# A seven-product step for half of the fourth column group of the down-projection, with sums made and split by halves

## The chip, the cores and the metric

The kernel runs on one core of a Trainium2 chip. The metric is the device time of one execution in microseconds (us), the median of several executions. In the profile PE is the matrix engine, PEld its weight loads, DVE the vector engine, ACT the scalar engine, POOL and SP the engines that here mostly issue transfers (DMAs).

## The reference

Two layers over 256 tokens of width 2048, in float32. The part that matters is the MLP at the end of each layer and the form of its products:

```python
for l in range(DEPTH):                       # DEPTH = 2, S = 256, D_MODEL = 2048, D_FF = 8192
    h = rms_norm(x, norm1_g[l])
    z = h @ w_in[l]                          # width 5120: q, k, v and two gMLP halves
    ...                                      # 8 attention heads, 8 gMLP groups -> mix
    x = x + mix @ w_out[l]
    h2 = rms_norm(x, norm2_g[l])
    x = x + jnp.square(jax.nn.relu(h2 @ w_up[l])) @ w_down[l]
return rms_norm(x, final_g)
```

## The kernel before

**Products.** Every float32 operand is split into a high part (a rounding to the matrix engine's fp32r type) and a low part (the remainder), and a product is made of three matmuls: high by high, low by high, high by low. A *weight tile* (class `Sub`) is 128 partitions x 1024 numbers: SP loads it (512 KB) into `raw`, ACT makes `hi` by a cast (L173), DVE makes `lo` by a subtraction (L183). A *plain* step (function `transposed`, matmuls of L415) uses one weight tile in 24 matmuls of 256 columns.

A *seven-product step* (function `fast`, matmuls of L443; the Strassen-Winograd form) takes four 256 x 256 blocks of weights, from two loaded tiles, `Top` and `Bottom`, and replaces two plain steps, 48 matmuls, by 42. For it DVE makes four weight differences of 128 x 512 (L224, L225, L228, L229), held in place of the raw tiles as two more tiles, `Sums`; these two get a cast and a low part like a plain tile (L173, L183), Top and Bottom a half-size cast (L191) and low part (L196) each. The matching combinations of the activations (`sum_parts`, kept in `shared`) are made once per eighth of the MLP: four DVE operations in `strassen_sums` (L485 to L488), then casts in `to_half` (ACT L661) and low parts (DVE L664).

**Stages.** The MLP is cut into eighths of 1024 hidden columns. Turn `e` of its loop (0 to 8), in the texts "eighth e", does the up-projection of eighth e, 16 plain steps numbered 0 to 15, and the down-projection of eighth e-1. After each four up steps ACT takes relu and square of 256 hidden columns (L888, L891) and casts them (L661), and DVE makes their low part (L664); so the last hidden columns of an eighth come at its step 15. The down-projection has four groups of 512 output columns. In eighths 1 to 6 three of them go by seven-product steps, two each (one per pair of row blocks of all 1024 rows), and the fourth by four plain steps, 16 to 19, whose results are added up in SBUF (L872, L875). In eighth 7 two groups are fast, in eighth 8 none.

**Results of the fast groups.** The seven products stay in PSUM for group 0; for the others ACT copies them out (three copies of 128 x 512, L1004, and one of 128 x 256, L990) and POOL's DMAs add them to the arrays `far` in DRAM (L969). In eighths 6 and 7 the last turn of a group is added the other way (L1000, L980 for group 0's seventh), `combine` adds the products up (seven DVE operations, L920 to L928, and ACT scalings, L933), `turn_back` turns each result on PE (four transposes, L945), and `update` adds it to `x` (L524).

**Order.** The program writes all engines' instructions from one list of steps. `ORDER` and `USUAL` say, per eighth and group, before which plain steps its fast steps stand. While step n is written, casts and low parts are written up to four tiles ahead (`high_to`, `low_to`); every engine runs its own instructions in the order written. A weight tile counts as a *unit*, so a fast step is four units; `soon`, `later` and `behind` put work off by units. PSUM banks are given in turn. The last two matmuls of a fast step are put into the next plain step.

## Time and profile before

| what | value |
|---|---|
| median of three runs | 2014.74 us (2014.72 to 2014.77) |
| profiled execution: own time, span | 2014.8 us, 2013.0 us |
| PE busy | 2000.5 us, 99% of the span, 16930 matmuls |
| DVE busy | 1659.6 us, 82%, 2116 instructions |
| ACT busy | 1259.3 us, 63%, 1695 instructions |
| bytes moved | 421.13 MB, mean 209 GB/s |

A line of instructions gives the start in us, the duration in us (of a run of several, from the first start to the last end), engine, line of the kernel, operation, output and inputs by name, shapes and count, then in brackets the idle time before it and what ended it. Durations of neighbours overlap, so what one instruction costs its engine is the distance from its start to the next one's, called pitch here. The windows view gives busy time and, in parentheses, instructions per engine, then the granted clock of PE.

### The profile page before, as it was taken

The numbers are of one execution on the slowest core, as the hardware profiler recorded it, in microseconds if no ns is written. First come the engines' busy times: TensorE is split into PE (matmuls) and PEld (weight loads), VectorE is DVE, ScalarE is ACT, GpSimd is POOL, SyncE is SP. The second block draws the span as 40 slices with busy tenths as digits, with TensorE's granted clock in tenths as the row PEclk, the third lists the DMA queues.
The fourth block names the chain that finished last, engine by engine and source line by source line (L and its number), as shares of the span: only waits on it lengthen the run. The fifth ranks groups of instructions, "written<-read, shape, count | busy, mean of one in ns | idle before, by whom it ended". The sixth has DMA issues, their size and how long they took to land.

```text
span 2013.0 us, 41185 instructions
## 1 busy us (share of the span) xinstructions
PE 2000.5 (99%) x16930; PEld 1971.9 (98%) x16930; DVE 1659.6 (82%) x2116; ACT 1259.3 (63%) x1695; POOL 136.8 (7%) x166
## 2 busy tenths in 40 slices
PE   9999999999999999999999999999999999999997
PEld 7999999999999999999989999999999999999997
DVE  7886866889888898898868877668888898888985
ACT  7666555676666666665647665556666666667653
POOL 0000300000001000100000003000001100010000
PEclk9999999999999999999999999999999999999998
DMA  8555556576678776876656456555677777778662
GB/s 325 199 170 166 189 191 208 165 263 211 206 230 241 242 222 202 245 218 214 201 176 209 167 173 196 189 193 180 240 233 218 231 235 216 235 223 251 200 215 82
DMA packets 127597, 421.13 MB, mean 209 GB/s; under 512 B 14256, under 2 KB 22448, under 8 KB 127408
## 3 DMA queue, kind: packets, MB, share of 16 engines
q1 hardware_dynamic: 110800, 389.86, 56.9%
q0 software_dynamic: 15456, 25.70, 7.1%
q8 instruction: 132, 2.16, 0.4%
q10 hardware_dynamic: 1152, 2.94, 0.4%
q14 instruction: 57, 0.47, 0.1%
HBM read 394.58 MB, written 23.86 MB: 208 GB/s over the span
## 4 chain that ended last, share of the span: by engine, by line
PE 99%; DMA 0%; DVE 0%; ACT 0%; ACTq 0%; issue 0%; DVEq 0%; SPq 0%
PE acc L415 69%; PE acc L443 12%; PE aux L443 9%; PE acc L475 2%; PE acc L474 2%; PE acc L473 2%; PE aux L772 0%; PE aux L650 0%; PE aux L608 0%; DMA raw<-in_w 0%; PE aux L637 0%; DMA x<-in_xT 0%; DVE x L1140 0%; PE aux L652 0%; PE acc L945 0%; PE aux L553 0%
## 5 line engine op out<-in xcount | busy, mean ns | idle before, releaser
L173 ACT ACTIVATE hi<-raw 128x1024 fp32r<-128x1024 f32 (+1 forms) x829 | 845.2, 1049 | 441.8 <-DVE raw L225 265.6
L183 DVE TENSOR_TENSOR lo<-raw,hi 128x1024 fp32r<-128x1024 f32 (+1 forms) x829 | 978.7, 1213 | 108.5 <-ACT hi L173 104.3
L415 PE MATMUL acc<-hs,hi 128*128 128x256 f32 x5632 | 988.6, 277 | 0.0
L415 PEld LDWEIGHTS acc<-hs,hi 128*128 128x128 f32 x5632 | 858.6, 188 | 0.4 <-issue 0.2
L415 PE MATMUL acc<-hs,lo 128*128 128x256 f32 x2816 | 778.0, 276 | 0.0
L415 PEld LDWEIGHTS acc<-hs,lo 128*128 128x128 f32 x2816 | 528.7, 188 | 0.4 <-issue 0.2
L415 PE MATMUL acc<-half,hi 128*128 128x256 f32 x2560 | 440.5, 276 | 0.0
L415 PEld LDWEIGHTS acc<-half,hi 128*128 128x128 f32 x2560 | 387.2, 188 | 0.0
L415 PE MATMUL acc<-half,lo 128*128 128x256 f32 x1280 | 353.3, 276 | 0.0
L415 PEld LDWEIGHTS acc<-half,lo 128*128 128x128 f32 x1280 | 240.3, 188 | 0.0
L969 POOL DMA_DIRECT2D far<-ar x100 | 80.9, 814 | 1138.1 <-ACT ar L972 519.2
L443 PE MATMUL acc<-hi,shared 128*128 128x256 f32 x832 | 149.9, 276 | 0.0
L443 PEld LDWEIGHTS acc<-hi,shared 128*128 128x128 f32 x832 | 129.1, 188 | 0.0
L443 PE MATMUL aux<-hi,half 128*128 128x256 f32 x608 | 126.4, 276 | 0.0
L443 PE MATMUL acc<-lo,shared 128*128 128x256 f32 x416 | 114.8, 276 | 0.0
L664 DVE TENSOR_TENSOR half<-ar,half 128x512 fp32r<-128x512 f32 x72 | 49.8, 691 | 63.7 <-ACT half L661 63.7
L443 PEld LDWEIGHTS aux<-hi,half 128*128 128x128 f32 x608 | 100.1, 188 | 0.0
L443 PE MATMUL acc<-hi,half 128*128 128x256 f32 x480 | 91.4, 276 | 0.0
L443 PE MATMUL aux<-lo,half 128*128 128x256 f32 x304 | 84.1, 277 | 0.0
L443 PE MATMUL aux<-hi,shared 128*128 128x256 f32 x448 | 80.7, 276 | 0.0
L524 DVE TENSOR_TENSOR x<-x,acc 128x512 f32<-128x512 f32 (+1 forms) x45 | 30.3, 674 | 58.9 <-PE acc L415 57.4
L443 PEld LDWEIGHTS acc<-lo,shared 128*128 128x128 f32 x416 | 78.1, 188 | 0.0
(181 smaller groups left out, 2113.4 us busy)
## 6 DMA issues: line engine op xcount, KB each, us to landing
raw<-in_w SPq DMA_DIRECT2D x731, 512.0 KB, 4.7
far<-ar POOLq DMA_DIRECT2D x66, 256.0 KB, 8.4
far<-ar POOLq DMA_DIRECT2D x34, 128.0 KB, 4.6
ar<-far POOLq DMA_DIRECT2D x12, 256.0 KB, 9.7
raw<-in_w SPq DMA_DIRECT2D x10, 256.0 KB, 5.0
x<-in_xT SPq DMA_DIRECT2D x7, 256.0 KB, 5.6
out<-x SPq DMA_DIRECT2D x7, 256.0 KB, 3.1
shared<-in_b_sp ACTq DMA_DIRECT2D x2, 512.0 KB, 7.5
```

Of the source, the lines that this page charges most:

```text
L173: act.activation(self.h[:, j * m:(j + 1) * m], self.raw[:, j * m:(j + 1) * m], AF.Copy)
L183: vec.tensor_tensor(lo[:, r], self.raw[:, r], self.h[:, r].bitcast(F32), op=OP.subtract)
L415: pe.matmul(o, lhsT=lhs, rhs=xs[:, rhs, :], start=(first and j == 0), stop=(last and j == 2), skip_group_check=True)
L443: calls.append(lambda k=k, j=j, lhs=lhs, rhs=rhs: pe.matmul(o[n], lhsT=lhs, rhs=rhs, start=(p == 0 and k == 0 and j == 0 and n in fresh), ...
L473: pe.matmul(ps, lhsT=xh, rhs=hi, start=(k0 + k == 0), stop=False)
L474: pe.matmul(ps, lhsT=xh, rhs=lo, start=False, stop=False)
L475: pe.matmul(ps, lhsT=xl, rhs=hi, start=False, stop=(k0 + k == KC - 1))
L524: vec.tensor_tensor(xj, xj, ps[j][:, 0:S] if alone else pair(ps)[:, j, :], op=OP.add)
L664: vec.tensor_tensor(t[:, c:c + 2, 1, :], src, t[:, c:c + 2, 0, :].bitcast(F32), op=OP.subtract)
L969: nc.gpsimd.dma_start(far[g][:, r], src, **({} if e == 1 else {"accum_op": OP.add}))
```

## The change

In eighths 1 to 5 the fourth group (output columns 1536 to 2047) is split by rows: the first 512 of the 1024 rows go by one seven-product step, before plain step 11, and the other 512 by two plain steps, 16 and 17, in place of four. For this the rows are paired in another way: a seven-product step now covers 512 neighbouring rows (top 256, bottom 256), and so does each half of the activation sums.

- The sums of the first half are made after step 8, and their casts and low parts behind the fast step that stands before plain step 14 (in eighth 6 before step 12); those of the second half follow step 15. Every low part of them is written one unit after its cast. Eighth 7's sums, which no step read, are no longer made.
- The hidden columns' first pair of blocks (of eighths 0 to 4) is cast and split for half of the tokens alone, since no plain step reads it any more.
- The products of the new step go out like those of group 1 and 2, into a fourth array `far[3]`, in eighths 1 to 5. In eighth 7, after group 0, one transfer of 128 x 1792 (0.92 MB) brings it into the tile `shared`; then come one `combine` and two `turn_back`s more per layer. The load of `far[0]` and group 0's `combine` stand four units later than before.
- The raw tiles are one tile with seven places, and the first two of the four weight differences become one operation of 128 x 1024 numbers; Bottom's low part stands behind it. Where a Top would take the last place, it and its Bottom change places.
- Group 2's fast steps stand before steps 14 and 15 (before: 13 and 14), and eighth 1 has the usual order.

The diff, cut to what matters:

```diff
@@ -60,10 +60,10 @@
-ORDER = {1: ((2, 5), (7, 8), (13, 14)), 6: ((12, 15), (2, 3), (7, 8)), 7: ((7, 10), (2, 3)), 8: ()}
-FINAL = (7, 7, 6)
+ORDER = {6: ((12, 15), (2, 3), (7, 8)), 7: ((7, 10), (2, 3)), 8: ()}
+FINAL = (7, 7, 6, 8)
 LAST = (4, 6, 8, 10, 0, 2, 12, 14)
-USUAL = ((7, 9), (2, 3), (13, 14))
+USUAL = ((7, 9), (2, 3), (14, 15), (11,))
@@ -147,6 +147,9 @@
+    raws = wp.tile([P, 1024 * RAW_BUFS], F32, name="raws")
@@ -158,7 +161,9 @@
         def load(self, parts):
-            self.raw = wp.tile([P, 1024], F32, name="raw", tag="raw", bufs=RAW_BUFS)
+            self.at = raw_at[0] % RAW_BUFS
...
+            self.raw = raws[:, 1024 * self.at:1024 * (self.at + 1)]
@@ -221,10 +226,13 @@
             if not self.second:
-                vec.tensor_tensor(t.left(), t.right(), t.left(), op=OP.subtract)
-                vec.tensor_tensor(t.right(), b.right(), t.right(), op=OP.subtract)
+                low_to(n_high[0] - 1)
+                o = t.raw.rearrange("p (k h n) -> p h k n", k=2, h=2)
+                right = raws.rearrange("p (s k h n) -> p s k h n", k=2, h=2, n=256)[:, t.at:b.at + 1:b.at - t.at, :, 1, :]
+                vec.tensor_tensor(o, right, o, op=OP.subtract)
...
             if not self.second:
+                low_to(n_high[0])
@@ -416,33 +424,33 @@
-    def fast(name, l, row0, col0, forms, slots, fresh, last, done):
+    def fast(name, l, row0, col0, forms, slots, fresh, last, done, count=2):
         o = []
-        for p in range(2):
-            top, bottom = (cls(name, l, row0 + (4 * h + 2 * p) * P, col0, 2, 512) for h, cls in enumerate((Top, Bottom)))
+        for p in range(count):
+            top, bottom = (cls(name, l, row0 + (4 * p + 2 * h) * P, col0, 2, 512) for h, cls in enumerate((Top, Bottom)))
...
                     o.extend(slots())
-                half, extra = forms()
+                half, extra = forms(p)
...
                     for k in range(2):
-                        xh, xl = (a[:, 4 * lower_rows + 2 * p + k, i, tt * P:(tt + 1) * P] for i in range(2))
+                        xh, xl = (a[:, 4 * p + 2 * lower_rows + k, i, tt * P:(tt + 1) * P] for i in range(2))
...
                                 o[n], lhsT=lhs, rhs=rhs, start=(p == 0 and k == 0 and j == 0 and n in fresh),
-                                stop=(n in last and p == 1 and k == 1 and j == 2), skip_group_check=True))
+                                stop=(n in last and p == count - 1 and k == 1 and j == 2), skip_group_check=True))
@@ -479,9 +487,12 @@
-    def strassen_sums(f, i, n):
...
-        a11, a12, a21, a22 = (f[:, 4 * k + i:4 * k + i + n, t * P:(t + 1) * P] for t in range(2) for k in range(2))
+    def strassen_sums(f, p=None):
...
+        f = f.rearrange("p (a r k) t -> p a r k t", a=2, r=2)
+        f = f if p is None else f[:, p:p + 1]
+        a11, a12, a21, a22 = (f[:, :, r, :, t * P:(t + 1) * P] if p is None else f[:, 0, r, :, t * P:(t + 1) * P]
+                              for t in range(2) for r in range(2))
@@ -656,12 +667,13 @@
-        def to_half(t, c, src, wait=False):
...
-            act.activation(t[:, c:c + 2, 0, :], src, AF.Copy)
+        def to_half(t, c, src, wait=False, n=S):
...
+            act.activation(t[:, c:c + 2, 0, 0:n], src[:, :, 0:n], AF.Copy)
             def low():
-                vec.tensor_tensor(t[:, c:c + 2, 1, :], src, t[:, c:c + 2, 0, :].bitcast(F32), op=OP.subtract)
+                vec.tensor_tensor(t[:, c:c + 2, 1, 0:n], src[:, :, 0:n], t[:, c:c + 2, 0, 0:n].bitcast(F32),
+                                  op=OP.subtract)
@@ -889,29 +901,33 @@
                 act.activation(z, z, AF.Square)
-                to_half(hid[e][0], c // P, z, True)
-                if e == 0 and c == 512:
+                to_half(hid[e][0], c // P, z, True, P if e < 5 and c == 0 else S)
+                if e == 0 and c == 256:
...
                     sum_parts[0] = shared[0].rearrange("p (k h t) -> p k h t", k=NH, h=2)
-                    later(1, 1.0, lambda: sums([0]))
-                if c == 768:
-                    summed[0] = False
-                    later(1, 1.5, lambda: sums([0, 1] if e else [1]))
+                if c % 512 == 256 and e < 7:
+                    if c == 768:
+                        later(1, 1.0, lambda: strassen_sums(inner, 1))
+                        parts(1, 1)
+                    elif e == 0:
+                        later(1, 1.0, lambda: strassen_sums(inner, 0))
+                        parts(0, 1)
...
-        def sums(ps):
...
-            strassen_sums(inner, 2 * ps[0], 2 * len(ps))
...
-            def parts(k):
-                to_half(sum_parts[0], k, inner[:, k:k + 2, :])
-                summed[0] = k == 6
...
-            for k in range(0, 8, 2):
-                if k % 4 // 2 in ps:
-                    later(0, 0.6, lambda k=k: parts(k))
...
-        def combine(place, c, banks, o=None):
+        def parts(p, wait):
+            summed[p] = wait is None
...
+            def part(k):
+                to_half(sum_parts[0], k, inner[:, k:k + 2, :], True)
+                summed[p] = summed[p] or k % 4 == 2
...
+            for k in (4 * p, 4 * p + 2):
+                if wait is None:
+                    part(k)
+                else:
+                    later(wait, 0.6, lambda k=k: part(k))
...
+        def combine(place, c, banks, o=None, between=2):
@@ -935,7 +951,7 @@
             soon(wait, lambda: turn_back(c, d2, d4, banks[0]))
-            soon(wait + (1 if o else 2), lambda: turn_back(c + 2, d3, d7, banks[1]))
+            soon(wait + (1 if o else between), lambda: turn_back(c + 2, d3, d7, banks[1]))
@@ -977,8 +993,10 @@
                 else:
-                    soon(10, lambda: nc.gpsimd.dma_start(stage[:, 1536:1792], far[0]))
-                    soon(15, lambda: combine(stage, 0, [aux_bank] * 2, o))
+                    soon(4, lambda: (new_shared(F32), nc.gpsimd.dma_start(shared[0][:, 0:1792], far[3])))
+                    soon(7, lambda: combine(shared[0], 12, [lambda i=i: acc_bank(i) for i in (2, 3)], None, 1))
+                    soon(14, lambda: nc.gpsimd.dma_start(stage[:, 1536:1792], far[0]))
+                    soon(19, lambda: combine(stage, 0, [aux_bank] * 2, o))
@@ -1011,17 +1029,19 @@
             if e < 8:
-                up = collect(transposed, "w_up", l, 0, KC, e * 1024, 1024, from_hs, after_up(e), of=2,
-                             cols=None if e else (0, 512, 256, 768))
+                up = collect(transposed, "w_up", l, 0, KC, e * 1024, 1024, from_hs, after_up(e), of=2)
             if e:
-                w = 512 * len(ORDER.get(e, USUAL))
+                w = 512 * min(len(ORDER.get(e, USUAL)), 3)
+                half = 0 < e < 6
...
-                def forms(tile=hid[e - 1]):
-                    sums_ready()
+                def forms(p, tile=hid[e - 1]):
+                    sums_ready(p)
...
-                down = collect(transposed, "w_down", l, (e - 1) * 1024, 8, w, D - w, from_tiles(hidden, NH),
+                rows = from_tiles(hidden, NH)
+                down = collect(transposed, "w_down", l, (e - 1) * 1024 + 512 * half, 8 - 4 * half, w, D - w,
+                               (lambda k, rows=rows: rows(k + 4)) if half else rows,
@@ -1030,12 +1050,16 @@
                                              (0, 2, 4, 6) if g or e == 1 else (6,), range(7) if g or e == 7 else (6,),
-                                             other_done(e, g, banks) if g else first_done(e)))
+                                             other_done(e, g, banks) if g else first_done(e), len(at)))
...
                 steps.append(one)
+                if 0 < e < 7 and i == 8:
+                    hook(len(steps) - 1, lambda: later(1, 0.6, lambda: strassen_sums(inner, 0)))
+                if 0 < e < 7 and i == max(at[0] for at in ORDER.get(e, USUAL)):
+                    hook(len(steps) - 1, lambda: parts(0, None))
@@ -1055,27 +1079,28 @@
     n_load, n_high, n_low, n_raw = [0], [0], [0], [0]
+    to_load = [u for u in subs if u.loads]
+    for i in range(RAW_BUFS - 1, len(to_load) - 1, RAW_BUFS):
+        if isinstance(to_load[i], Top):
+            sums = [u for u in subs if isinstance(u, Sums) and u.top is to_load[i]]
+            sums[0].frees, sums[1].frees = 0, 2
+            to_load[i:i + 2] = to_load[i + 1], to_load[i]
...
     def load_more():
-        while n_load[0] < len(subs):
-            if not subs[n_load[0]].loads:
-                n_load[0] += 1
-                continue
+        while n_load[0] < len(to_load):
...
                 nc.sync.dma_start(x[:, c:c + 2, :], xv[:, c:c + 2, :])
-            subs[n_load[0]].load(2 if n_load[0] < HALVES else 1)
+            to_load[n_load[0]].load(2 if n_load[0] < HALVES else 1)
...
-            if not subs[n_high[0]].loads:
-                low_to(n_high[0] - subs[n_high[0]].second)
...
```

**The matrix engine's counts.** Matmuls of L415 go from 12288 to 11808, those of L443 from 3696 to 4116, transposes of `turn_back` from 48 to 64.

On DVE, at the boundary of eighths 4 and 5 of the first layer, before (`lo`, `hi` are split weights, `half` split hidden columns, `ar` hidden columns or running sums, `shared` split activation sums):

```order
L664 TENSOR_TENSOR half<-ar,half 128x2x256
L485 TENSOR_TENSOR ar<-ar 128x4x128
L486 TENSOR_TENSOR ar<-ar 128x4x128
L487 TENSOR_TENSOR ar<-ar 128x4x128
L488 TENSOR_TENSOR ar<-ar 128x4x128
L183 TENSOR_TENSOR lo<-raw,hi 128x1024
L875 TENSOR_TENSOR ar<-ar,acc_8521 128x512
L664 TENSOR_TENSOR shared<-ar,shared 128x2x256 x2
L196 TENSOR_TENSOR lo<-raw,hi 128x512
L664 TENSOR_TENSOR shared<-ar,shared 128x2x256 x2
L183 TENSOR_TENSOR lo<-raw,hi 128x1024
L224 TENSOR_TENSOR raw<-raw 128x2x256
```

The same place in the changed kernel, from the low part of the last hidden columns:

```order
L675 TENSOR_TENSOR half<-ar,half 128x2x256
L887 TENSOR_TENSOR ar<-ar,acc_8372 128x512
L496 TENSOR_TENSOR ar<-ar 128x2x128
L497 TENSOR_TENSOR ar<-ar 128x2x128
L498 TENSOR_TENSOR ar<-ar 128x2x128
L499 TENSOR_TENSOR ar<-ar 128x2x128
L232 TENSOR_TENSOR raws<-raws 128x2x2x256
L188 TENSOR_TENSOR lo<-raws,hi 128x1024
L236 TENSOR_TENSOR raws<-raws 128x2x256
L237 TENSOR_TENSOR raws<-raws 128x2x256
L675 TENSOR_TENSOR shared<-ar,shared 128x2x256
L887 TENSOR_TENSOR ar<-ar,acc_8412 128x512
```

Between the last hidden columns and the fast step of group 1 that follows stand now one addition to the running sums (L887, was L875), sums of half the size, and already the weight differences of that fast step; the two low parts of the second half's sums (L675, was L664) come after them, and the second L887 behind the first of these.

On POOL, in eighths 6 and 7 of the first layer, before:

```order
L1000 DMA ar<-far_89 128x512 x3
L1000 DMA ar<-far_89 128x256
L969 DMA far_87<-ar 128x256
L1000 DMA ar<-far_88 128x512 x3
L1000 DMA ar<-far_88 128x256
L980 DMA ar<-far_87 128x256
```

and in the changed kernel:

```order
L1018 DMA ar<-far_90 128x512 x3
L1018 DMA ar<-far_90 128x256
L985 DMA far_88<-ar 128x256
L1018 DMA ar<-far_89 128x512 x3
L1018 DMA ar<-far_89 128x256
L996 DMA shared<-far_91 128x1792
L998 DMA ar<-far_88 128x256
```

The load of `far[3]` (here far_91) stands ahead of the load of group 0's seventh product, on the same engine.

More of the change, by code (lines that the diff above doesn't have):

```diff
@@ L454, in mm @@
                 left_over.extend(calls[-BEHIND:])
-            steps.append(((top, bottom, upper, lower), mm, (lambda: done(o)) if p and done else None))
+            steps.append(((top, bottom, upper, lower), mm, (lambda: done(o)) if p == count - 1 and done else None))
     def natural(name, l, col0, ncols, after):
@@ L706, in seven_forms @@
         def seven_forms(rows):
-            return lambda: (hs[:, NH * rows:NH * (rows + 1)], seven["sums"])
+            return lambda p: (hs[:, NH * rows:NH * (rows + 1)], seven["sums"])
         def seven_plain(rows, i):
@@ L816, in layer @@
             hook(base + 11 + i, lambda i=i: seven_plain(0, i))
[L817 removed]
+        hook(base + 13, lambda: strassen_sums(seven["plain"][0]))
         for k in range(0, NH, 2):
@@ L959, in slots_other @@
         def slots_other(g, banks):
-            seventh = sevenths()[g - 1]
+            seventh = sevenths()[(g - 1) % 2]
             banks[:] = [acc_bank(1 - bank_at[0]), acc_bank(2), acc_bank(3)]
             return [h for b in banks for h in halves(b)] + [seventh]
-        far = [dp.tile([P, 256 if g == 0 else 7 * 256], F32, name=f"far{l}{g}") for g in range(3)]
+        far = [dp.tile([P, 256 if g == 0 else 7 * 256], F32, name=f"far{l}{g}") for g in range(4)]
         def put(e, g, r):
```

15 lines of the change are left out of this document (8 added, 7 removed).

## The prediction

> **What bounds the kernel now.** I read the page first: the busy shares and the chain of work that ended last (its shares by engine).
>
> ```profile
> PE 2000.5 (99%) x16930; PEld 1971.9 (98%) x16930; DVE 1659.6 (82%) x2116; ACT 1259.3 (63%) x1695; POOL 136.8 (7%) x166
> PE 99%; DMA 0%; DVE 0%; ACT 0%; ACTq 0%; issue 0%; DVEq 0%; SPq 0%
> ```
>
> PE is the chain. Next the waits of PE, all that there are, and the windows view of one eighth of the first layer's MLP (us, PE, PEld, DVE, ACT, POOL, granted clock, DMA share, GB/s).
>
> ```profile
> PE aux L333 <- DVE nr L359: 1.2, 1, 1.2
> PE aux L1096 <- DVE warm L1092: 1.1, 1, 1.1
> PE acc L473 <- ACT hs L292: 0.3, 1, 0.3
> 622.80:705.90 83.10, 83.10 (x734) 83.10 (x733) 72.78 (x83) 54.80 (x69) 7.82 (x9) 1.00 0.73 227
> ```
>
> None of these waits (2.6 us in all) is in an MLP eighth. So time falls by the matmuls that PE no longer runs, as long as DVE and ACT, which make the weights' parts, still deliver each in time. One matmul of 256 columns costs 83.10/734 = 0.1132 us at clock 1.00. DVE is busy 72.78 of 83.10 us: there is room, but not much. What decides is whether DVE is late at one place.
>
> **Terms of the sum.** (1) A seven-product step runs 42 matmuls for 48. The counts in the order of the instructions are 480 fewer of L415 and 420 more of L443, five eighths in two layers: 60 fewer, 60 x 0.1132 = **-6.79 us**.
>
> (2) The new `turn_back`s add 16 transposes in four groups. What one group costs shows where one stands in a plain step now (PE timeline, eighth 6):
>
> ```profile
> 863.68 0.28 PE L415 MATMUL acc<-half,hi 128*128 128x256 f32 x1
> 863.79 0.60 PE L945 MATMUL acc<-con,ar 128*128 128x128 f32 x4
> 864.15 0.37 PE L415 MATMUL acc<-half,hi 128*128 128x256 f32 x1
> 864.36 0.28 PE L415 MATMUL acc<-half,lo 128*128 128x256 f32 x1
> ```
>
> Between the starts of the first row and the last lie two matmuls of 256 columns, 0.23 us; it takes 0.68: the group costs 0.45, four of them **+1.80 us**. Sum: -4.99, so the profiled 2014.8 becomes 2009.8 (and the span 2013.0 becomes 2008.0). The profiled execution is within 0.06 us of the median 2014.74, so nothing is added for that.
>
> (3) Vector and scalar work, at nothing if PE covers it. DVE's prices are pitches, at the boundary of eighths 4 and 5:
>
> ```profile
> 697.08 0.69 DVE L664 TENSOR_TENSOR half<-ar,half 128x512 fp32r<-128x512 f32 x1 [0.76 <-ACT half L661]
> 697.80 0.69 DVE L485 TENSOR_TENSOR ar<-ar 128x512 f32<-128x512 f32 x1
> ...
> 699.98 0.69 DVE L488 TENSOR_TENSOR ar<-ar 128x512 f32<-128x512 f32 x1
> 700.59 1.22 DVE L183 TENSOR_TENSOR lo<-raw,hi 128x1024 fp32r<-128x1024 f32 x1
> 701.73 0.68 DVE L875 TENSOR_TENSOR ar<-ar,acc 128x512 f32<-128x512 f32 x1
> 702.33 1.28 DVE L664 TENSOR_TENSOR shared<-ar,shared 128x512 fp32r<-128x512 f32 x2
> 703.53 0.68 DVE L196 TENSOR_TENSOR lo<-raw,hi 128x512 fp32r<-128x512 f32 x1
> ...
> 706.47 0.68 DVE L224 TENSOR_TENSOR raw<-raw 128x512 f32<-128x512 f32 x1
> 707.19 0.69 DVE L225 TENSOR_TENSOR raw<-raw 128x512 f32<-128x512 f32 x1
> 707.92 0.69 DVE L228 TENSOR_TENSOR raw<-raw 128x512 f32<-128x512 f32 x1
> 708.64 0.69 DVE L229 TENSOR_TENSOR raw<-raw 128x512 f32<-128x512 f32 x1
> 709.25 0.68 DVE L875 TENSOR_TENSOR ar<-ar,acc 128x512 f32<-128x512 f32 x1
> ...
> 852.92 0.43 DVE L923 TENSOR_TENSOR ar<-ar 128x256 f32<-128x256 f32 x1
> 853.38 0.43 DVE L924 TENSOR_TENSOR ar<-ar 128x256 f32<-128x256 f32 x1
> 853.72 0.42 DVE L925 TENSOR_TENSOR ar<-ar 128x256 f32<-128x256 f32 x1
> ```
>
> A 512-wide operation costs 0.60, or 0.73 where the next one reads its result (L485 to L488: 2.79 for four); a 1024-wide low part 1.14 (1.25 by its duration where the next must wait for it); a 256-wide one 0.46 or 0.34, so four sums in a row 3 x 0.46 + 0.34 = 1.72, and two halves 3.44 in place of 2.79. The one operation that no row shows is the merged difference of 128 x 1024. Lower bound: 1.14, a 1024-wide operation of the same kind (L183); upper: 1.45, no gain over L224 and L225. I take 1.14: it is a subtraction of as many float32 numbers as L183's. An eighth of 1 to 5 then gains on DVE the new step's 2 x 0.60 + 2 x 1.14 + (1.14 + 0.73 + 0.61) = 5.96, and 0.65 of split sums, and loses two plain low parts, 2.28, six times 0.31, and 0.14 of half a chunk: 75.1 busy of 726 x 0.1132 = 82.2 us. On average it is covered.
>
> For the merged form the Trainium skill has a price, in "VectorE: DVE Perf Modes", section "The TRN2 errata — SBUF-src ops pay a fixed extra latency per instruction": a float32 two-tensor addition takes (N+151)/0.96 ns. That gives an estimate of 1.22 us of duration for 1024 and 0.69 for 512, as the rows of L183 and L224 have it. By it, too, the split of the sums is a loss (0.42 for each 256-wide part).
>
> **The tight place** is the boundary of two eighths, where the last hidden columns must pass through ACT and DVE. The order puts the fast step of group 2 right before step 15, so ACT and PE start together behind it, as at the plain step after the same fast step now (PE's last matmul of it, ACT's casts), and I build the chain from there. The last three rows show, at the second fast step of group 1, when DVE starts the low part of its third tile, when PE starts the step, and when it asks for that part.
>
> ```profile
> 689.46 0.28 PE L443 MATMUL aux<-hi,half 128*128 128x256 f32 x1
> 689.47 4.84 ACT L173 ACTIVATE hi<-raw 128x1024 fp32r<-128x1024 f32 x5
> 695.11 0.60 ACT L888 ACTIVATE ar<-acc 128x512 f32<-128x512 f32 x1 [0.53 <-PE acc L415]
> 695.74 0.64 ACT L891 ACTIVATE ar<-ar 128x512 f32<-128x512 f32 x1
> 696.41 0.64 ACT L661 ACTIVATE half<-ar 128x512 fp32r<-128x512 f32 x1
> 699.98 1.15 ACT L661 ACTIVATE shared<-ar 128x512 fp32r<-128x512 f32 x2 [1.47 <-DVE ar L487]
> 717.77 4.79 DVE L183 TENSOR_TENSOR lo<-raw,hi 128x1024 fp32r<-128x1024 f32 x4
> 718.73 0.28 PE L443 MATMUL acc<-hi,half 128*128 128x256 f32 x1
> 720.89 0.28 PE L443 MATMUL acc<-lo,shared 128*128 128x256 f32 x1
> ```
>
> From t = 0 PE runs steps 15, 16, 17, 0, 1 (5 x 24 x 0.1133 = 13.60), the first fast step of group 1 to 18.36, plain step 2 to 21.08, and asks for the second fast step's low part at 21.08 + 2.16 = 23.24. ACT: three casts at 0.95 and a half one at 0.53 to 3.38, relu 0.63, square 0.67, cast and DVE's start 0.67: DVE begins the last low part at 5.35. Then, in the order shown: low part 0.60, L887 0.60, four sums 1.72, merged difference 1.14, Bottom's low part 1.25, two differences 1.34, a low part of the sums 0.60: 12.60. The second L887, 0.68, ends at 13.28. It frees the PSUM bank that the first fast step takes at 13.60: **0.32 us to spare**. On DVE goes on to the second fast step (1.14, 0.60, 2.28, 0.60, 1.14, 1.25, 1.34, and its low part 1.22): about 22.9 against 23.24, **0.35 to spare**. Before the change the same low part is made from 717.77 to 718.99 and used at 720.89, 1.9 us ahead. So the change eats nearly all the room at this place, in eighths 2 to 5, eight times in the two layers; elsewhere it leaves more. I take no stall, and what lies above 0.35 goes into the range: each us more on this chain costs some 0.65 x 8 = 5 us.
>
> **The big transfer.** In eighth 7 `far[3]` is loaded (917,504 B) into `shared`, which PE last reads at 918.4, and DVE runs into `combine` behind the last hidden columns' low part at about 927. Rows of today: PE's last read, DVE there, the lead of the next low part over PE, and landings (us, median).
>
> ```profile
> 918.38 0.28 PE L443 MATMUL aux<-hi,shared 128*128 128x256 f32 x1
> 926.90 0.69 DVE L664 TENSOR_TENSOR half<-ar,half 128x512 fp32r<-128x512 f32 x1 [0.24 <-ACT half L661]
> 928.10 2.35 DVE L183 TENSOR_TENSOR lo<-raw,hi 128x1024 fp32r<-128x1024 f32 x2
> 939.26 0.28 PE L415 MATMUL acc<-half,lo 128*128 128x256 f32 x1
> raw<-in_w SPq DMA_DIRECT2D x731, 512.0 KB, 4.7
> ar<-far POOLq DMA_DIRECT2D x12, 256.0 KB, 9.7
> ```
>
> The first low part of the pair is done by 929.3 and used at 939.3: 10 us ahead. `combine` itself takes 7 operations, 5 x 0.46 + 2 x 0.34 = 3.0. PE starves only if the load lands over 8.5 + 10 - 3 = 15.5 us after 918.4. Bounds: 4.7 (as a weight load of half the size) and 3.5 x 9.7 = 34 us (if it goes at the rate of the adding loads, one after another). It adds nothing to what it reads, so I take the near end, 5 to 10 us: hidden. Queued behind it on POOL are only `far[0]`'s load and later ones, moved four units later. The Trainium skill, "DMA: Bandwidth & Descriptors", section "Anatomy of one DMA — SWDGE (gpsimd) path", gives 2.0 us plus bytes/436e3, an estimate of 4.1 us alone; by that it is hidden as well.
>
> ACT gets two half casts more (its two casts of differences take the place of two plain ones) and four copies an eighth, six operations at about a cast's 0.53, some 3 us of the 28 idle in an eighth (83.10 - 54.80). SP loads as many tiles as before.
>
> **Rivals.** *B, DVE is late at the boundary by a few tenths.* For: the margins of 0.32 and 0.35 are sums of some twenty pitches, and the merged difference stands in the chain twice. With it at 1.45 the first margin is 0.01, the second -0.27: a stall of 0.3 at eight places, 2.4 us, and 0.2 more elsewhere: 2012.4. If the whole chain is a microsecond longer, 5 us are lost, 2014.8, the time of before. Against: pitches come from neighbouring rows with one clock, and PE has no such stall now.
>
> *C, the other side: the load of `far[3]` lands late.* One place per layer, the wait of DVE's first `combine` operation; low parts behind it are stuck, and PE stops. From 15.5 us of landing on every us costs one per layer. At 34 us: 2 x 18.5 = 37 us, 2009.8 + 37 = 2047. For: the adding loads of a quarter of the size take 9.7. Against: those read, add and write; a plain one has half or less.
>
> **Chances.** The forecast (no stall over 0.1 us a place) 0.60, B 0.33, C 0.07. A measurement of this kernel can tell about 0.2%, 4 us, from no change: below 2010.7 is faster. The forecast's own range is 2009.3 to 2010.7 (0.5 below for transposes that overlap better). B falls between 2010.7 and 2014.8, mostly near 2012.4, so it counts as the same; C is slower. For 8 in 10 the range takes the forecast and the near half of B, to 2013.4. So faster 0.60, same 0.33, slower 0.07.
>
> **What would show it.** In the changed profile: 60 fewer matmuls and 16 more transposes; still no wait of PE on DVE in L423 or L451. Merged differences of about 1.22 us at L232. In a boundary, the end of the second L887 0.3 us ahead of the first fast step, and the low part of the second fast step 0.3 us ahead of its use. The first `combine` operation of eighth 7 with no idle time on a DMA before it. The forecast is wrong if PE's waits show acc or lo at L451 in eighths 2 to 5 (B), or DVE sits idle on the DMA of `shared` (C), or if the transposes of the new groups cost more than 0.45 each.

## The result, and the profile after

| | time, us (median, lowest to highest) |
|---|---|
| before | 2014.76 (2014.72 to 2015.14, 4 runs) |
| changed | 2034.61 (2033.95 to 2034.82, 4 runs) |
| ratio | 1.0098 [1.008, 1.0115] |

The change made the kernel slower by 20 us, where I forecast 5 us less (2009.8, range 2009.3 to 2013.4). The page of the changed kernel (busy us, share of the span, instructions), its rows for the merged difference and for the transfer of `far[3]`, and all waits of PE:

```profile
PE 2019.9 (99%) x16886; PEld 1991.3 (98%) x16886; DVE 1694.2 (83%) x2128; ACT 1286.1 (63%) x1755; POOL 169.8 (8%) x208
L232 DVE TENSOR_TENSOR raws<-raws 128x1024 f32<-128x1024 f32 x98 | 119.9, 1224 | 2.8
shared<-far POOLq DMA_DIRECT2D x2, 896.0 KB, 7.5
PE aux L341 <- DVE nr L367: 1.2, 1, 1.2
PE aux L1121 <- DVE warm L1117: 1.1, 1, 1.1
PE acc L482 <- DVE lo L188: 0.9, 1, 0.9
```

PE runs 44 matmuls fewer (60 less, 16 transposes more), as counted, the big transfer lands in 7.5 us, and PE has no listed wait in the MLP. By waits nothing is wrong, and yet PE is busy 19 us longer. The windows view says where: 50 us of the same part of the MLP, before and after, and in each the stretch of the MLP of which I speak below (us, PE with its number of matmuls, PEld, DVE, ACT, POOL, granted clock, DMA share, GB/s).

```profile
600.00:650.00 50.00, 50.00 (x443) 50.00 (x442) 44.09 (x51) 34.56 (x45) 6.96 (x8) 1.00 0.76 229
545.00:862.00 317.00, 317.00 (x2796) 317.00 (x2795) 279.20 (x316) 211.98 (x269) 30.53 (x35) 1.00 0.75 229
```

```profile
600.00:650.00 50.00, 50.00 (x427) 50.00 (x426) 46.50 (x54) 36.14 (x50) 7.31 (x9) 1.00 0.80 233
544.40:873.60 329.20, 329.20 (x2798) 329.20 (x2797) 297.00 (x330) 224.47 (x292) 41.11 (x47) 1.00 0.77 231
1550.10:1879.80 329.70, 329.70 (x2799) 329.70 (x2798) 296.97 (x331) 224.63 (x293) 40.55 (x47) 1.00 0.77 231
```

Before, 443 matmuls start or run in 50 us, after, 427 (a count takes in some two that only reach into the window): 113.4 against 117.7 ns from one to the next, at the same granted clock of 1.00. I call these the short and the long pitch. The long one lasts from 544.4 to 873.6 in the first layer and from 1550 to 1880 in the second. At the short pitch 2796 matmuls take 317.0 us; the two stretches of 329.2 and 329.7 with 2798 and 2799 therefore cost about 24.3 us, and 2034.6 - 24.3 = 2010.3 is near what I had forecast. The added matmuls and copies don't explain it; a stretch of 330 us with a longer pitch does, and it starts at one matmul. PE, its weight loads and DVE around that matmul:

```profile
544.29 0.28 PE L423 MATMUL acc<-hs,lo 128*128 128x256 f32 x1
544.40 0.28 PE L423 MATMUL acc<-hs,hi 128*128 128x256 f32 x1
544.52 0.30 PE L451 MATMUL acc<-hi,half 128*128 128x256 f32 x1
544.65 0.28 PE L451 MATMUL acc<-lo,half 128*128 128x256 f32 x1
```

```profile
544.29 0.19 PEld L423 LDWEIGHTS acc<-hs,hi 128*128 128x128 f32 x1
544.42 0.19 PEld L451 LDWEIGHTS acc<-hi,half 128*128 128x128 f32 x1
544.53 0.19 PEld L451 LDWEIGHTS acc<-lo,half 128*128 128x128 f32 x1
```

```profile
543.09 0.68 DVE L675 TENSOR_TENSOR shared<-ar,shared 128x512 fp32r<-128x512 f32 x1
543.69 0.68 DVE L887 TENSOR_TENSOR ar<-ar,acc 128x512 f32<-128x512 f32 x1
544.29 1.22 DVE L188 TENSOR_TENSOR lo<-raws,hi 128x1024 fp32r<-128x1024 f32 x1
```

It is the tight place of the prediction: the first fast step of group 1 in eighth 3 takes the bank that the second L887 frees. L887 ends at 544.37; the step's first weight load starts at 544.42, 0.13 us after the one before it, not 0.11: it waited some 0.02 us. That is too short to be listed as a wait. The stretch ends with the transposes of eighth 6:

```profile
873.02 0.28 PE L423 MATMUL acc<-half,hi 128*128 128x256 f32 x1
873.14 0.60 PE L961 MATMUL acc<-con,ar 128*128 128x128 f32 x4
873.50 0.37 PE L423 MATMUL acc<-half,hi 128*128 128x256 f32 x1
873.70 0.28 PE L423 MATMUL acc<-half,lo 128*128 128x256 f32 x1
```

**Theory:** a wait of PE, however short, can change the pitch at which its weight loads and matmuls follow each other, and the long pitch then stays until something sets it back. **Rival:** the changed kernel's work in eighths 3 to 6 (more transfers, more DVE and ACT work on the same memory) slows PE, and the wait is incidental.

The Trainium skill, "TensorE: Matmul & The Clock Gate", section "What's actually happening", knows two states of PE's clock, half and full. A pitch 3.8% longer is neither, and the rows' clock of 1.00 on both sides agrees that the gate is not the cause. The Trainium skill has, in the section "Back-to-back issue gap" of the same page, the spacing of matmuls in a stream set by weight load and matmul together, and 262 cycles (an estimate of 109 ns) for a matmul of 256 columns by itself. The traces have 113.4 and 117.7, two values for the same pair.

### The profile page after: what moved, and what is told of

It is laid out like the page before. It is cut to its first block, busy times and chain, and to the rows that moved or that the text cites. A ratio compares the mean times of both kernels' runs of the same rounds, so it can differ in the third digit from the quotient of the medians.

```text
span 2032.8 us, 41330 instructions
## 1 busy us (share of the span) xinstructions
PE 2019.9 (99%) x16886; PEld 1991.3 (98%) x16886; DVE 1694.2 (83%) x2128; ACT 1286.1 (63%) x1755; POOL 169.8 (8%) x208
## 4 chain that ended last, share of the span: by engine, by line
PE 99%; DMA 1%; DVE 0%; ACT 0%; ACTq 0%; issue 0%; SPq 0%; DVEq 0%
PE acc L423 67%; PE acc L451 14%; PE aux L451 10%; PE acc L482 2%; PE acc L483 2%; PE acc L481 2%; PE aux L784 0%; PE aux L661 0%; PE aux L619 0%; DMA raws<-in_w 0%; PE acc L961 0%; PE aux L648 0%; DVE x L1165 0%; DMA x<-in_xT 0%; PE aux L663 0%; PE aux L564 0%
## 5 line engine op out<-in xcount | busy, mean ns | idle before, releaser
L178 ACT ACTIVATE hi<-raws 128x1024 fp32r<-128x1024 f32 (+1 forms) x839 | 860.8, 1049 | 453.6 <-DVE raws L232 167.9
L188 DVE TENSOR_TENSOR lo<-raws,hi 128x1024 fp32r<-128x1024 f32 (+1 forms) x839 | 994.0, 1213 | 112.6 <-ACT hi L178 107.8
L423 PE MATMUL acc<-half,hi 128*128 128x256 f32 x2240 | 388.6, 277 | 0.0
L423 PEld LDWEIGHTS acc<-half,hi 128*128 128x128 f32 x2240 | 340.1, 188 | 0.0
L423 PE MATMUL acc<-half,lo 128*128 128x256 f32 x1120 | 309.7, 277 | 0.0
L423 PEld LDWEIGHTS acc<-half,lo 128*128 128x128 f32 x1120 | 210.5, 188 | 0.0
L985 POOL DMA_DIRECT2D far<-ar x140 | 113.3, 888 | 1121.4 <-ACT ar L1022 614.2
L451 PE MATMUL acc<-hi,shared 128*128 128x256 f32 x992 | 182.7, 278 | 0.0
L451 PEld LDWEIGHTS acc<-hi,shared 128*128 128x128 f32 x992 | 155.1, 188 | 0.0
L451 PE MATMUL acc<-lo,shared 128*128 128x256 f32 x496 | 137.8, 278 | 0.0
L451 PE MATMUL aux<-hi,half 128*128 128x256 f32 x648 | 137.2, 278 | 0.0
L232 DVE TENSOR_TENSOR raws<-raws 128x1024 f32<-128x1024 f32 x98 | 119.9, 1224 | 2.8
L451 PE MATMUL acc<-hi,half 128*128 128x256 f32 x560 | 108.7, 278 | 0.0
L451 PEld LDWEIGHTS aux<-hi,half 128*128 128x128 f32 x648 | 107.3, 188 | 0.0
L451 PEld LDWEIGHTS acc<-lo,shared 128*128 128x128 f32 x496 | 93.0, 188 | 0.0
L451 PE MATMUL aux<-lo,half 128*128 128x256 f32 x324 | 90.1, 278 | 0.0
L451 PEld LDWEIGHTS acc<-hi,half 128*128 128x128 f32 x560 | 90.0, 188 | 0.0
L451 PE MATMUL aux<-hi,shared 128*128 128x256 f32 x448 | 82.4, 278 | 0.0
```

The costliest lines, as they stand in the source:

```text
L178: act.activation(self.h[:, j * m:(j + 1) * m], self.raw[:, j * m:(j + 1) * m], AF.Copy)
L188: vec.tensor_tensor(lo[:, r], self.raw[:, r], self.h[:, r].bitcast(F32), op=OP.subtract)
L232: vec.tensor_tensor(o, right, o, op=OP.subtract)
L423: pe.matmul(o, lhsT=lhs, rhs=xs[:, rhs, :], start=(first and j == 0), stop=(last and j == 2), skip_group_check=True)
L451: calls.append(lambda k=k, j=j, lhs=lhs, rhs=rhs: pe.matmul(o[n], lhsT=lhs, rhs=rhs, start=(p == 0 and k == 0 and j == 0 and n in fresh), ...
L985: nc.gpsimd.dma_start(far[g][:, r], src, **({} if e == 1 else {"accum_op": OP.add}))
```

## The experiments

### One short wait in the kernel before

The cleanest test leaves all of the changed kernel's work out and adds one wait to the kernel before.

```diff
+WAITS = {(0, 2): (9, 54), (1, 2): (7, 60)}      # (layer, eighth): how many, how wide
...
             else:
+                if c == 14 and (l, e) in WAITS:
+                    n, m = WAITS[l, e]
+                    for i in range(n):
+                        o = ones[:, 64 * (i % 2):64 * (i % 2) + m]
+                        vec.tensor_tensor(o, o, o, op=OP.mult)
                 y = rest_sums[:, c - 12:c - 10, :]
                 vec.tensor_tensor(y, y, pair(ps), op=OP.add)
```

> The kernel before with nine small multiplications on DVE (128 x 54, 1.16 us in all) ahead of the second L875 at the end of eighth 2 of the first layer, so that PE's first fast step of eighth 3 waits some 0.02 to 0.05 us for its bank, once in the whole execution; in the second layer seven of 128 x 60, 0.95 us, at the same place, which leaves 0.2 us to spare, no wait. Theory (cadence): PE at 117.7 ns from there to the transposes of eighth 6, some 2800 matmuls x 4.35 ns = 12 us, in the first layer only: 2026.9. Rival (contention in the changed kernel, waits cost their length): 2014.8.

2026.85 us as the median of seven runs (ratio 1.0053 [1.0038, 1.0068]); six lie between 2026.78 and 2027.28, one at 2014.86. In the profiled one PE's first matmul of the fast step (545.33) is followed 0.17 us later by the second, a wait of under 0.06 us, and then the layers differ:

```profile
545.22 0.28 PE L416 MATMUL acc<-hs,hi 128*128 128x256 f32 x1
545.33 0.33 PE L444 MATMUL acc<-hi,half 128*128 128x256 f32 x1
545.50 0.28 PE L444 MATMUL acc<-lo,half 128*128 128x256 f32 x1
...
600.00:650.00 50.00, 50.00 (x426) 50.00 (x426) 42.30 (x49) 33.08 (x42) 6.05 (x7) 1.00 0.69 209
1600.00:1650.00 50.00, 50.00 (x443) 50.00 (x442) 41.95 (x49) 32.61 (x42) 5.40 (x7) 1.00 0.66 209
```

426 matmuls per 50 us in the layer with the wait, 443 in the other, with the traffic of before in both. One wait of 0.06 us cost 12 us. The rival falls: the changed kernel's work is not needed for the long pitch. The seventh run was not profiled: either PE met no wait in it, or the wait left the pitch short, as some waits below do.

### Waits of graded length

```diff
+SWEEP = {(0, 2): (8, 64), (0, 3): (9, 54), (0, 4): (9, 58), (0, 5): (9, 64),
+         (1, 2): (10, 63), (1, 3): (12, 62), (1, 4): (16, 60), (1, 5): (23, 61)}
...
+    def turns():
+        ps = acc_bank(2)
+        for j in range(4):
+            pe.transpose(ps[:, j * P:(j + 1) * P], con[:, j * P:(j + 1) * P], ident)
...
                 steps.append(one)
+                if 3 <= e <= 6 and i == 6:      # second run: i == 4, other lengths
+                    hook(len(steps) - 1, turns)
```

The multiplications stand in the same loop as before, with `SWEEP` for `WAITS`.

> The kernel before, with waits of PE of graded length. At the ends of eighths 2 to 5 small multiplications of ones by ones (in place, 128 x 54 to 64, 8 to 23 of them) stand ahead of the second addition to the running sums (L875), which frees the bank of the next fast step, with 1.14 us to spare at all eight places; they delay it by about 1.12, 1.16, 1.20, 1.26 us in the first layer and 1.39, 1.65, 2.17, 3.14 us in the second, so PE should wait about 0 (no wait), 0.02, 0.06, 0.12, 0.25, 0.5, 1.0 and 2.0 us. Four transposes of a constant tile after plain step 6 of the next eighth follow each. Theory (cadence): after waits of some of these lengths, the short ones at least, PE runs at 117.7 ns until the transposes, and at 113.4 after the place without a wait; some 3.6 us for transposes, 4 for the waits and 0.8 for each flip: 2023 to 2028. Rival (contention from the changed kernel's traffic): 113.4 ns everywhere, since the traffic is that of before: 2022.

2042.07 us (one run). The first step of the scale, meant as no wait, already delayed PE by 0.01 us in the first layer, and PE went to the long pitch; my added transposes did not set it back, so the following waits of that layer tell nothing:

```profile
600.00:650.00 50.00, 50.00 (x426) 50.00 (x426) 43.36 (x58) 32.96 (x42) 6.09 (x7) 1.00 0.68 208
1820.00:1870.00 50.00, 50.00 (x442) 50.00 (x442) 44.02 (x49) 34.96 (x45) 7.00 (x8) 1.00 0.86 257
```

In the second layer the first wait (0.26 us in all) brought the long pitch, one of 0.4 kept it, and the last, of 1.3 us, set the short one back: the second row lies behind it.

> As the run sweep, the kernel before with waits of graded length, but with the four transposes after plain step 4 of eighths 3 to 6, where they set PE back (run turns4), so that the eight waits are told apart. The multiplications on DVE take about 1.19, 1.23, 1.31, 1.47 us in the first layer and 1.65, 1.91, 1.39, 2.17 in the second, so PE should wait some 0.05, 0.09, 0.17, 0.33, 0.5, 0.77, 0.25 and 1.0 us. Theory (cadence): most of them leave PE at 117.7 ns until the transposes; each such flip costs some 160 matmuls x 4.35 ns = 0.7 us where the transposes set it back: 2014.7 + 3.6 + 3.2 + up to 5.6 = 2022 to 2027, more where they do not.

2033.59 us (one run). Here the transposes, followed by a plain step, set the pitch back, but for one group in the first layer (eighth 5), and seven of the eight waits met PE at the short pitch. From the starts of PE's matmuls in the timeline:

| wait, us (sum of the two delayed starts) | layer, after eighth | pitch behind it |
|---|---|---|
| 0.08 | first, 2 | long |
| 0.11 | first, 3 | long |
| 0.19 | first, 4 | long |
| 0.52 | second, 2 | long |
| 0.77 | second, 3 | long |
| 0.25 | second, 4 | short |
| 1.02 | second, 5 | short |

So the length alone does not decide. The wait of 0.25 us left no trace in the pitch, one of 0.19 did. The 16 us behind the waits of 0.52 and 0.25 us:

```profile
1556.00:1572.00 16.00, 16.00 (x138) 16.00 (x137) 14.43 (x16) 10.72 (x15) 2.61 (x3) 1.00 0.75 225
1726.00:1742.00 16.00, 16.00 (x143) 16.00 (x143) 14.83 (x17) 10.70 (x14) 2.61 (x3) 1.00 0.73 229
```

### Setting the pitch back by transposes in the changed kernel

```diff
+    def turns():                                # the same function
...
+                if 3 <= e <= 6 and i == 6:      # run turns; run turns4: i == 4
+                    hook(len(steps) - 1, turns)
                 if 0 < e < 7 and i == 8:
```

> The changed kernel with four more transposes of a constant tile (128 x 128 float32, into the PSUM bank of acc2, read by nobody) after plain step 6 of eighths 3, 4, 5 and 6 in both layers. They cost 8 x 0.45 = 3.6 us. Theory (cadence): as the transposes of eighth 7 do, they set PE back to 113.4 ns; then it is slow only from the first fast step of an eighth to plain step 6, some 180 matmuls x 4.3 ns = 0.8 us, where a wait of 0.02 us flips it again: about 2010 + 3.6 + 8 x 0.8 = 2020. Rival (contention or a lowered clock in these eighths): 2034.6 + 3.6 = 2038, PE at 117.7 ns on both sides of the added transposes.

2038.21 us (2 runs): 2034.6 + 3.6, as the rival had it, since the added transposes before a fast step left PE at the long pitch.

> As the run turns, but with the four added transposes after plain step 4 of eighths 3 to 6, where a plain step follows, as one follows the transposes of eighth 6 that set PE back; in the run turns a fast step followed and PE stayed slow. If what follows the transposes decides: PE is set back each time and flipped at each boundary again, slow for some 160 matmuls eight times, 2010 + 3.6 + 8 x 0.7 = 2019. If the added transposes can't set it back: 2038 as before.

2023.74 us (2021.01 to 2024.00, 3 runs): 11 us less than the changed kernel, with 3.6 us of work added. 50 us behind the transposes of eighth 3, in the run turns and then in turns4:

```profile
571.00:621.00 50.00, 50.00 (x427) 50.00 (x426) 43.77 (x48) 34.23 (x46) 6.99 (x8) 1.00 0.73 221
```

```profile
564.00:614.00 50.00, 50.00 (x443) 50.00 (x442) 45.07 (x51) 32.86 (x43) 5.31 (x7) 1.00 0.77 232
```

At seven of the eight boundaries a wait of 0.02 us for the bank met PE at the short pitch, and each time the long one followed. In the first layer one group of the four (eighth 5) failed to set PE back; that is some 730 matmuls x 4.35 ns = 3 us of the 5 that the profiled execution (2024.0) took over the expectation. The other 2 lie outside the MLP, where the 110 us from 1090 hold 822 matmuls, against 842 in the changed kernel at the same place (from 1094); why the pitch was long there is not known. The long pitch in the changed kernel is therefore a state of PE, not of the work around it: the same eighth runs at either.

### Taking away what makes PE wait

First the order of two DVE operations: the low parts of the second half's sums one unit later, so that L887 frees the bank 0.6 us earlier.

```diff
-                behind.append((now[0] + 1, low))
+                behind.append((now[0] + wait, low))
-                to_half(sum_parts[0], k, inner[:, k:k + 2, :], True)
+                to_half(sum_parts[0], k, inner[:, k:k + 2, :], 1 if wait is None else 2)
```

> The changed kernel with one difference in DVE's order: the low parts of the second half's sums (L675) are written two units after their casts, not one, so that the second L887, which frees the PSUM bank for the first fast step of group 1, stands one 0.60 us operation earlier. Theory (cadence): in the changed kernel PE's weight load at 544.425 waited 0.02 us for that L887, and this flips PE from 113.4 to 117.7 ns per matmul until the transposes of eighth 7, 2797 matmuls x 4.3 ns = 12 us a layer. With the bank free 0.6 us early the flip at this place goes: some 2010 us if no other wait of the kind is behind it; the third tile's low part of the second fast step has a margin of only about 0.02 to 0.1 us in a kernel without the flip, so a flip there, some 66 matmuls later, would leave it at about 2034. Rival (contention: the added traffic of eighths 3 to 6 slows PE): still 2034, with 117.7 ns in the same eighths and no wait at their start.

Four runs, two near 2029.6 and two near 2048.4, ratio 1.012 [1.0071, 1.017]. The wait at the bank went, but the later low parts now stopped PE in eighth 1, once in each layer:

```profile
PE acc L451 <- DVE shared L675: 1.1, 2, 0.5
600.00:650.00 50.00, 50.00 (x443) 50.00 (x442) 47.82 (x54) 36.08 (x49) 7.88 (x9) 1.00 0.81 241
1600.00:1650.00 50.00, 50.00 (x427) 50.00 (x426) 46.50 (x52) 36.65 (x50) 6.93 (x8) 1.00 0.78 231
```

Two waits of the same kind and length (0.81 us in both layers, as the sum of two delayed starts): after the one the pitch is short, after the other long. A long pitch from eighth 1 on costs 4166 matmuls x 4.35 ns = 18 us, the distance between the two pairs of runs; the upper pair then had it in both layers, which is inferred, since it was not profiled. The first layer shows the changed kernel's eighths 2 to 6 at the short pitch with all their work.

The same for eighths 1 to 6 alone:

```diff
-                to_half(sum_parts[0], k, inner[:, k:k + 2, :], True)
+                to_half(sum_parts[0], k, inner[:, k:k + 2, :], 2 if wait and turn else 1)   # turn: the eighth
```

> As swap, the low parts of the second half's sums two units after their casts, but in eighths 1 to 6 alone; eighth 0 keeps the changed kernel's order, so the 0.7 us wait of PE for such a low part in eighth 1, which the run swap added in both layers (and which left PE fast in one layer and slow in the other), should be gone. Theory (cadence): no wait in the eighths, PE at 113.3 ns throughout, 2009.8 (my forecast's count of matmuls and transposes), faster than before by 5 us. Rival (contention by the changed kernel's work): the bulk of the 20 us stays, since the work is the same.

2018.94 us (11 runs), ratio 1.002 [1.0011, 1.0029]. The first layer is at the short pitch throughout; in the second, one wait remains, at the fourth tile's low part of the second fast step:

```profile
1628.96 1.22 DVE L188 TENSOR_TENSOR lo<-raws,hi 128x1024 fp32r<-128x1024 f32 x1
1630.53 2.36 DVE L188 TENSOR_TENSOR lo<-raws,hi 128x1024 fp32r<-128x1024 f32 x2 [0.36 <-ACT hi L178]
```

```profile
1631.52 0.39 PE L451 MATMUL acc<-hi,shared 128*128 128x256 f32 x2
1631.81 0.39 PE L451 MATMUL acc<-lo,shared 128*128 128x256 f32 x1
```

PE starts 0.07 us late at 1631.81 and the matmul behind it 0.11 late (0.18 as a sum of two delayed starts), and the remaining 1972 matmuls to the transposes take 8.6 us more. Then the steps themselves were moved, three times:

```diff
-USUAL = ((7, 9), (2, 3), (14, 15), (11,))
+USUAL = ((7, 9), (2, 3), (13, 14), (11,))       # early
+USUAL = ((7, 9), (2, 3), (13, 14), (10,))       # early10
+USUAL = ((7, 9), (3, 4), (14, 15), (11,))       # shift, with 6: ((12, 15), (3, 4), (7, 8)); shift2: from swap2
```

> The changed kernel with the two fast steps of group 2 before plain steps 13 and 14, where they stood before the change, not 14 and 15; all else is kept. DVE then starts the boundary chain from step 15's end, about 0.6 us earlier against the fast steps of group 1, and both margins grow by about 0.6 us. Theory (cadence): no wait, PE at 113.4 ns throughout, about 2010 us. Rival (contention): as much work and traffic as the changed kernel, so 2034.

2056.49 us, ratio 1.0207 [1.019, 1.0224]. I overlooked that group 2's step at 13 takes the bank of steps 8 to 11, which ACT frees (L900) only behind its casts:

```profile
PE acc L451 <- ACT ar L900: 11.2, 10, 1.3
```

Ten waits, 13.9 us as sums of delayed starts (1.57 for the first of a layer, 1.34 for each of the others), and the long pitch from the first of them, in eighth 1, on: some 3770 matmuls x 4.35 ns x 2 = 33 us. The eight waits of 1.34 us met PE at the long pitch and left it there.

> The changed kernel with group 2's fast steps before plain steps 13 and 14 and the new step before step 10 (in the run early it stayed at 11, and PE waited 1.4 to 1.6 us per eighth for the banks that ACT had to copy out). Three plain steps then lie between the new step and group 2's as in the changed kernel, and the boundary chain starts 0.8 us earlier. Theory (cadence): no wait, 2009.8. If three plain steps beside the closer steps 9 and 10 are not enough, a wait at step 10 or 13 of the first such eighth flips PE for the rest of the MLP: 2040 to 2050. Rival (contention): 2034.

2047.75 us, ratio 1.0164 [1.015, 1.0178]. The list shows two such waits, and the pitch is long from the first of them on, as in the run early:

```profile
PE acc L451 <- ACT ar L900: 1.8, 2, 0.9
```

The matmuls' starts show eight more, of some 0.35 us each, which the list leaves out; with the two of 1.19 that is 5.2 us. For both kernels 2010 us, the waits and the long pitch add up to within 1 us of what they take.

> The changed kernel with group 1's two fast steps before plain steps 3 and 4, not 2 and 3, in eighths 1 to 6 (nothing else moved). Both tight waits of the boundary, for the bank and for the third tile's low part of the second fast step, then come due one plain step, 2.72 us of PE, later, while DVE has one low part more, 1.14, in front: 1.6 us more room at each. Theory (cadence): no wait, PE at 113.4 ns, 2009.8, 5 us less than before. A new wait could come at steps 7 and 9, since only three plain steps lie between step 4's fast step and step 7's; then 2015 or more, with the slow cadence behind it. Rival (contention by the changed kernel's traffic): 2030 or more, slow in eighths 3 to 6.

2019.56 us as the median of eleven runs, spread from 2014.12 to 2027.22, ratio 1.0021 [1.0009, 1.0032]. The boundary has room, but the first matmul of plain step 4 now asks for a bank that the fast step right before it has filled and ACT copies out (L1022) a little late:

```profile
640.89 1.55 ACT L1022 ACTIVATE ar<-acc 128x512 f32<-128x512 f32 x3
```

```profile
641.61 0.30 PE L423 MATMUL acc<-hs,hi 128*128 128x256 f32 x1
641.75 0.28 PE L451 MATMUL aux<-lo,half 128*128 128x256 f32 x1
```

A few hundredths of a us (641.75 comes 0.14 after 641.61, where 0.12 is usual), and the long pitch from there on. That it strikes first in another eighth from run to run would explain the spread; one execution was profiled.

> swap2 with group 1's fast steps before 3 and 4 in eighths 1 to 5 alone; eighth 6 keeps 2 and 3. In swap2 one wait of 0.07 us was left, on the third tile's low part of the second fast step of group 1 (second layer, eighth 4), and it cost 8.6 us. Theory (cadence): that wait goes; what is left is the same place in eighth 6, some 60 us ahead of the transposes that set PE back: 2009.8 without a flip, 2012.5 with one in one layer.

2019.92 us (2015.94 to 2027.29, 10 runs), ratio 1.0024 [1.0013, 1.0035]: the same wait at step 4. In eighth 4 a wait of 0.03 us there left the short pitch as it was, in both layers; at the same step of eighth 5 PE waited 0.35 us (two delayed starts) in both layers, and went to the long pitch in the first, not in the second:

```profile
725.00:775.00 50.00, 50.00 (x427) 50.00 (x426) 45.11 (x50) 31.94 (x42) 7.42 (x9) 1.00 0.83 239
1725.00:1775.00 50.00, 50.00 (x443) 50.00 (x442) 46.56 (x50) 32.75 (x43) 6.80 (x8) 1.00 0.80 235
```

In the second layer the long pitch came in eighth 6, where the expectation allowed for it: PE waited 0.18 us at 1801 for the third tile's low part, 62 us ahead of the transposes. (In swap2 it was the fourth tile's, as the rows above show, not the third's.)

### A version without the wait

The last kernel keeps all of the change and of swap2, and takes one more low part out of the chain: the one for the upper rows of the second half's sums, which PE reads late, goes behind the third tile's low part of the step that uses it.

```diff
+    pending = []
+            upper.releases = p == 1
-            if wait:
-                behind.append((now[0] + 1, low))
+            if wait is pending:
+                pending.append(low)
+            elif wait:
+                behind.append((now[0] + wait, low))
-                to_half(sum_parts[0], k, inner[:, k:k + 2, :], True)
+                to_half(sum_parts[0], k, inner[:, k:k + 2, :], (2 if k == 6 else pending) if wait and turn else 1)
             subs[n_low[0]].low(parts)
+            if getattr(subs[n_low[0]], "releases", False):
+                while pending:
+                    pending.pop(0)()
```

> swap2 with one operation more moved: of the two low parts of the second half's sums, the one for the upper rows, which PE reads only in the fourth and fifth product of the second fast step, is written right behind that step's third low part instead of ahead of its whole chain; so that chain (Top's low part, merged difference, Bottom's low part, two differences, third low part) runs 0.6 us earlier. In swap2 PE was fast in the whole first layer and was flipped once, in the second, by a wait of 0.07 us at the fourth tile's low part of that step (ACT's cast was 0.27 us later there than elsewhere). With 0.6 us more at that place: no wait, PE at 113.4 ns in both layers. Theory (cadence): 2009.8 plus 0.5 at most, faster than before by 0.2%. Rival (contention by the changed kernel's work): 2018 or more.

**2010.20 us** (2009.67 to 2010.47, 10 runs), ratio to before 0.9976 [0.9966, 0.9985]: faster than both kernels, 4.7 us under before and 24 under the change.

```profile
PE 1995.9 (99%) x16886; PEld 1966.9 (98%) x16886; DVE 1692.5 (84%) x2128; ACT 1283.2 (64%) x1755; POOL 169.9 (8%) x208
600.00:650.00 50.00, 50.00 (x442) 50.00 (x442) 48.18 (x55) 36.09 (x49) 7.89 (x9) 1.00 0.82 241
1600.00:1650.00 50.00, 50.00 (x443) 50.00 (x442) 47.61 (x54) 35.54 (x47) 6.92 (x8) 1.00 0.80 254
```

The same 16886 matmuls, the same 2128 and 1755 operations of DVE and ACT as in the changed kernel, 82% of the DMA engines' time in the first window against 80%, and 24 us less: all of what the change lost was the pitch.

## Why the prediction was wrong, point by point

- **The sum of PE's work was right.** 60 matmuls fewer and 0.45 us per group of transposes (873.02 to 873.70, 0.68 as quoted before) gave 2009.8; the kernel with the same work and no wait takes 2010.2.
- **The prices of DVE's work were right.** The merged difference lasts 1.22 us, a low part's duration, as the lower bound had it (1.13 from its start to the next one's). From the last low part of the hidden columns to the end of the second L887 (544.37) the chain takes 7.93 us, just what I added up (5.35 to 13.28).

```profile
536.44 0.69 DVE L675 TENSOR_TENSOR half<-ar,half 128x512 fp32r<-128x512 f32 x1
```

- **Rival C did not come.** The load of `far[3]` lands in 7.5 us, within the 5 to 10 that I took, and PE has no wait for it.
- **The margin of 0.32 us was 0.34 too large.** Three parts of it are seen in the trace. ACT was 0.2 late: the casts of the first half's sums (L672) stand ahead of the copies (L1022), and its casts of weights behind them begin at 531.11, where the step of group 2 ends at 530.91 (the first fast step, without its wait, at 544.51, less 13.60).

```profile
527.70 1.13 ACT L672 ACTIVATE shared<-ar 128x512 fp32r<-128x512 f32 x2
528.73 1.05 ACT L178 ACTIVATE hi<-raws 128x1024 fp32r<-128x1024 f32 x1
529.68 1.55 ACT L1022 ACTIVATE ar<-acc 128x512 f32<-128x512 f32 x3
531.11 1.06 ACT L178 ACTIVATE hi<-raws 128x1024 fp32r<-128x1024 f32 x1
```

  I had taken their start from the kernel before, where no such casts stand there. PE asks for the bank at the weight load, 0.1 ahead of the matmul (544.42 and 544.52). And 0.05 us pass from L887's end to the start of the load. Together 0.35: 0.32 to spare became a wait of 0.02.
- **The second margin was 0.18, not 0.35.** The terms as quoted end at 22.8, not 22.9, since the next operation starts 0.60 behind the start of the second L887 and not at its end; that leaves 0.47. In the trace the third tile's low part starts at 552.75 and ends at 553.97, 23.06 behind 530.91. ACT's 0.2 is in it, and 0.12 at the half-size low part, which cost 0.72 (548.30 to 549.02), not 0.60. PE, slow by then, asked for it at 554.55, so nothing waited; at the short pitch it would have asked 23.24 behind 530.91, at 554.15. At this step swap2 and shift2 met their waits for low parts.
- **The step that failed is the price of a wait.** Rival B said "a stall of 0.3 at eight places, 2.4 us", and the sum said "each us more on this chain costs some 0.65 x 8 = 5 us": a wait was priced at its length. One wait of 0.02 us cost 12 us in each layer, because PE's pitch stayed 4.3 ns longer for 2800 matmuls. The place and the size of the overrun were within what rival B described. Its reason, a merged difference of 1.45 us, was not what happened, and its sign, a wait of PE at L451 in the list, did not show, since 0.02 us is not listed. The range ended at 2013.4 because no row of before shows PE waiting in an eighth, so none could show what a wait there does.
- **What is open.** Why PE has two pitches, and which waits bring the long one: waits from 0.01 to 1.6 us did, waits of 0.03, 0.25, 0.35, 0.8 and 1.0 us in other places did not. One wait of 1.3 us in the run sweep ended it, eight of that length in the run early did not. Transposes ended it where a plain step followed, with one failure in each of turns4 and sweep2, and not where a fast step followed.

## What to carry to other kernels

Where an engine runs for hundreds of microseconds without a gap, count its instructions per window before and after a change: a longer pitch at an unchanged clock appears in no list of waits. A margin that is a sum of twenty pitches and ends at 0.3 us is no margin; look for an operation that can move out of the chain (here one low part, read late) before adding work. And a time that varies from run to run, as in the runs swap and shift, can come from a wait that is met or missed by a few nanoseconds, or that changes the pitch only sometimes; here this is inferred, since one execution of each kernel was profiled.

## What the runs showed of the hardware that I had not expected

For pairs of weight load and 256-column matmul in float32 parts PE has two steady pitches, 113.4 and 117.7 ns, at a granted clock of 1.00, and keeps either for thousands of matmuls. The kernel before has short stretches of the long one too, outside the MLP: 78 matmuls are counted from 92 to 101 us, 81 in as many microseconds from 105 on.

```profile
92.00:101.00 9.00, 9.00 (x78) 9.00 (x78) 6.19 (x12) 6.98 (x17) 0.00 (x0) 1.00 0.56 178
105.00:114.00 9.00, 9.00 (x81) 9.00 (x80) 7.92 (x11) 3.08 (x5) 0.00 (x0) 1.00 0.59 177
```
